# Weight sums of the gates' seven-product units: by adding DMAs for the first two units only, on DVE for the later four

## The chip, the cores and the metric

One core of one Trainium2 chip runs the whole kernel. The metric is the device time of one execution in microseconds (us). The engines are TensorE (PE, with its weight loads PEld), VectorE (DVE), ScalarE (ACT), GpSimd (POOL, which here issues adding DMAs) and SyncE (SP, which issues the other DMAs).

## What is computed

One block of a network on 512 tokens with 1024 channels, in fp32. The change touches only how the two gates are projected, the last two cuts of `proj`:

```
h = rms_norm(x, norm1_g[l])
proj = h @ w_in[l]
u_x, u_g, q, k, v, g_r, g_a = jnp.split(proj, cuts, axis=-1)
...
merged = (jax.nn.sigmoid(g_r) * (y_rnn @ w_br_rnn[l])
          + jax.nn.sigmoid(g_a) * (y_attn @ w_br_attn[l]))
x = x + merged @ w_out[l]
h2 = rms_norm(x, norm2_g[l])
x = x + jnp.square(jax.nn.relu(h2 @ w_mlp1[l])) @ w_mlp2[l]
```

Every product is held transposed (channels on the 128 partitions, 512 tokens along the row). To keep fp32 precision each operand is split in a high and a low part, and a product is three matmuls (high by high, high by low, low by high).

## The kernel before

**Units.** After attention and the recurrent branch the work is a list of units (`units()`). A unit is a pair of output chunks of 128 channels, with 1 MB of weights that SP loads as `raw`, four blocks of 128x512. The list around the change is: gr 0 and gr 2 (plain), four rnn units, then ga 0, gr 4, att 0, ga 2, gr 6, att 2, ga 4, att 4, ga 6, att 6, and then the output projection and the MLP ("one" and "two"). ga and gr are the two gates, att and rnn their branches.

**Seven products.** A plain unit splits its four blocks and uses them as four pieces. The units ga 0, gr 4, ga 2, gr 6, ga 4 and ga 6, and 14 units of the MLP, work as a 2x2 block product with seven multiplications in place of eight (`seven_products`). They use seven pieces: four blocks and three sums of blocks. The sums start from two: s1 = block 2 + block 3, and block 2 = block 2 + block 0. Later DVE makes block 0 + s1 (L220) and block 1 + block 0 (L222).

**Who makes the first two sums.** In the MLP DVE does (L217, L218), as the first piece of the unit is made. For the six gate units `load_unit` (L186 to L200) lets transfers do it: SP copies block 2 into s1 (L198), POOL issues one adding DMA of block 3 into s1 (L199) and one of block 0 into block 2 of `raw` (L200):

```
s1 = self.sums[u] = self.side[:, :T]
self.nc.sync.dma_start(s1, src[:, 2 * T:3 * T])
self.nc.gpsimd.dma_start(s1, src[:, 3 * T:], accum_op=ALU.add)
self.nc.gpsimd.dma_start(raw[:, 2], src[:, :T], accum_op=ALU.add)
```

All six share one tile, `side` (its name in the trace is pT): 512 columns for s1 and 256 for `uu`, the running difference of the products.

**Order.** `make_piece` asks for the loads of its unit and of the next one; `raw` has two buffers. Pieces are made eight ahead of their use on PE, in a ring of eight: ACT writes the high part (`whi`, L203), DVE the low part (`wlo`, L204). Since the next unit's load is asked for when a unit's first piece is made, and `side` is one tile, the copy and the add for gr 6 stand ahead of ga 2's first read of s1 in the program. So L220 of ga 2 waits for both units' transfers, and reads what gr 6's left there; gr 4 follows ga 0 in the same way. In the PE order a unit's first products are mixed with its neighbours' matmuls. The engines' orders are set by a scheduler.

**Products and their readers.** `seven_products` puts its products into four PSUM banks, in two tiles. ACT copies the first into `uu` (L266). DVE then reads the others: L268 (`uu`), L270, L272, L276 and L278 (into the unit's result `z`, S in the trace). PE's fourth product waits for L270, the sixth for L272 and the seventh for L276, since they write the tile that these read. The fifth needs no DVE reader.

Of the kernel before, what the change touches and what calls it, by code (L numbers as in the profile page):

```python
# [14 lines left out]
P = 128  # L15
T = 512
# [76 lines left out]
class Build:  # L93
# [93 lines left out]
    def load_unit(self, u):  # L187
        if u < len(self.units) and u not in self.raw_u:
            raw = self.t("raw", (P, 4, T), bufs=2)
            src = self.a["wts"][P1_END // 2 + u]  # L190
            self.nc.sync.dma_start(raw.rearrange("p c f -> p (c f)"), src)
            self.raw_u[u] = raw
            if self.units[u][0] in ("gr", "ga") and self.units[u][3]:

                if self.side is None:
                    self.side = self.t("pT", (P, T + H2))
# [4 lines that stand above are left out]
# [5 lines left out]
    def make_piece(self):  # L206
        V, n = self.nc.vector, self.made
        u, j = self.pieces[n]
        self.load_unit(u)
        self.load_unit(u + 1)  # L210
        raw = self.raw_u[u]
        blk = [raw[:, i] for i in range(4)]
        if self.units[u][3]:

            if j == 0 and u not in self.sums:
                s1 = self.sums[u] = self.t("pT", (P, T))
                V.tensor_tensor(s1, blk[2], blk[3], op=ALU.add)  # L217
                V.tensor_tensor(blk[2], blk[2], blk[0], op=ALU.add)  # L218
            elif j == 1:
                V.tensor_tensor(blk[0], blk[0], self.sums[u], op=ALU.add)  # L220
            elif j == 6:
                V.tensor_tensor(blk[1], blk[1], blk[0], op=ALU.add)  # L222
            src = (blk[0], blk[0], blk[2], self.sums[u], blk[1], blk[3], blk[1])[j]
        else:
            src = blk[j]
        s, e = n // 2 % (self.RING // 2), n % 2
        if n < self.RING and e == 0:
            self.ring_h.append(self.t("whi", (P, 2, T), FR, bufs=4))
            self.ring_l.append(self.t("wlo", (P, 2, T), FR, bufs=4))
        hi, lo = self.ring_h[s][:, e], self.ring_l[s][:, e]  # L230
        self.split_to(src, hi, lo)
        self.piece[n] = [x.rearrange("p (k m) -> p k m", m=P) for x in (hi, lo)]
        self.made += 1
# [804 lines left out]
```

## Time and profile before

| | |
|---|---|
| median of 3 runs | 891.11 us (890.53 to 893.37) |
| the profiled execution | 890.41 us, of which the span is 888.6 us |
| PE busy | 869.9 us, 98% of the span |
| DVE busy | 617.8 us, 70%, 1063 instructions |
| ACT busy | 494.4 us, 56% |
| POOL busy | 17.9 us, 2%, 25 instructions |
| chain that ended last | PE 91%, DVE 3%, ACT 2%, DMA 2% |

The span is the time from the first to the last instruction that the profile shows; the execution has 1.8 us around it. PE is the bound nearly everywhere, so what counts is where PE stands still, and at which clock it runs. TensorE's clock has two levels here, 2.4 GHz (1.00 in the PEclk column) and 1.2 GHz (0.50).

### The profile page before, as it was taken

Reading aid. Unit: us, or ns where it says so; the run is one execution under the profiler, and the core shown is the slowest. Engines: PE = TensorE matmul, PEld = TensorE weight load, DVE = VectorE, ACT = ScalarE, POOL = GpSimd, SP = SyncE. Lnnn points to the kernel's source line nnn. Section 1 sums busy time; section 2 is a strip of 40 time slices with the busy share of each in tenths; the row PEclk is TensorE's granted clock in tenths of the full one; section 3 lists DMA queues with packets and bytes.
Section 4 is the critical chain, followed back from the end, with each engine's and each line's share of the span. In section 5 each row is a group of like instructions: output and inputs, shape, how many; then the busy total and the mean of one; then the engine's idle time right before and its main releaser. Section 6 shows DMA issues by size and latency. Waiting matters only on the chain.

```text
span 888.6 us, 13051 instructions
## 1 busy us (share of the span) xinstructions
PE 869.9 (98%) x5033; PEld 744.0 (84%) x5033; DVE 617.8 (70%) x1063; ACT 494.4 (56%) x925; POOL 17.9 (2%) x25
## 2 busy tenths in 40 slices
PE   9999999999999999979999999999999999999996
PEld 7887788788787788968888889888888888888996
DVE  7777787795986866646765897776666666666533
ACT  7544856957868964524444546654444444444532
POOL 0000000000000012010000000000000000000000
PEclk9999999999999999989999999999999999999998
DMA  8443233134231357253436221222222222322211
GB/s 285 149 143 115 66 90 122 56 104 128 72 119 60 107 143 201 77 137 120 131 107 237 95 95 49 95 96 95 95 95 96 98 104 108 108 104 96 96 49 47
DMA packets 25645, 97.54 MB, mean 110 GB/s; under 512 B 3568, under 2 KB 6896, under 8 KB 16624
## 3 DMA queue, kind: packets, MB, share of 16 engines
q1 hardware_dynamic: 22704, 91.48, 29.8%
q0 software_dynamic: 2880, 5.24, 3.5%
q8 instruction: 39, 0.64, 0.3%
q14 instruction: 22, 0.18, 0.1%
HBM read 86.23 MB, written 2.10 MB: 99 GB/s over the span
## 4 chain that ended last, share of the span: by engine, by line
PE 91%; DVE 3%; ACT 2%; DMA 2%; issue 1%; SPq 0%; POOL 0%; DVEq 0%; ACTq 0%
PE pmm L248 38%; PE psc L248 22%; PE pmm L166 7%; PE pmm L167 7%; PE pmm L168 6%; PE psc L453 2%; PE pmm L453 2%; PE pmm L597 2%; PE psc L543 2%; DMA pT<-wts 1%; DMA S<-X 1%; PE ptr L581 1%; ACT L345 1%; ACT L L345 1%; DMA L<-xT 1%
## 5 line engine op out<-in xcount | busy, mean ns | idle before, releaser
L203 ACT CAST whi<-raw 128x512 fp32r<-128x512 f32 (+1 forms) x236 | 144.4, 626 | 212.5 <-PE pmm L248 101.0
L204 DVE TENSOR_TENSOR wlo<-raw,whi 128x512 fp32r<-128x512 f32 (+1 forms) x236 | 162.4, 697 | 55.6 <-ACT whi L203 52.7
L248 PE MATMUL psc<-X,whi 128*128 128x256 f32 x592 | 113.4, 289 | 6.4 <-DVE S L276 5.9
L248 PEld LDWEIGHTS psc<-X,whi 128*128 128x128 f32 x592 | 92.6, 190 | 14.1 <-DVE S L276 7.1
L248 PE MATMUL pmm<-E,whi 128*128 128x512 f32 x256 | 82.1, 396 | 0.3 <-ACT rot L345 0.3
L248 PE MATMUL psc<-X,wlo 128*128 128x256 f32 x296 | 81.5, 282 | 0.0
L166 PE MATMUL pmm<-X,whi 128*128 128x512 f32 x200 | 80.9, 405 | 0.0
L248 PE MATMUL pmm<-L,whi 128*128 128x512 f32 x256 | 80.5, 396 | 0.0
L167 PE MATMUL pmm<-X,whi 128*128 128x512 f32 x200 | 79.2, 396 | 0.0
L168 PE MATMUL pmm<-X,wlo 128*128 128x512 f32 x200 | 79.2, 396 | 0.0
L248 PE MATMUL psc<-Q,whi 128*128 128x256 f32 x320 | 70.1, 286 | 0.8 <-DVE tmp L268 0.8
L248 PEld LDWEIGHTS psc<-Q,whi 128*128 128x128 f32 x320 | 52.3, 188 | 6.4 <-DVE tmp L268 3.2
L248 PEld LDWEIGHTS pmm<-L,whi 128*128 128x128 f32 x256 | 48.0, 188 | 11.4
L248 PE MATMUL pmm<-B,whi 128*128 128x512 f32 (+1 forms) x224 | 57.5, 345 | 0.0
L248 PEld LDWEIGHTS pmm<-E,whi 128*128 128x128 f32 x256 | 47.6, 188 | 9.8 <-ACT rot L345 0.5
L248 PEld LDWEIGHTS psc<-X,wlo 128*128 128x128 f32 x296 | 55.5, 190 | 0.0
L248 PE MATMUL pmm<-V,whi 128*128 128x512 f32 (+1 forms) x192 | 54.6, 363 | 0.0
L248 PE MATMUL pmm<-L,wlo 128*128 128x512 f32 x128 | 50.8, 397 | 0.0
L248 PE MATMUL pmm<-E,wlo 128*128 128x512 f32 x128 | 50.7, 396 | 0.0
L136 ACT CAST whi<-raw 128x1024 fp32r<-128x1024 f32 (+1 forms) x36 | 34.3, 955 | 28.3 <-PE pmm L167 22.0
L166 PEld LDWEIGHTS pmm<-X,whi 128*128 128x128 f32 x200 | 37.7, 188 | 10.4 <-issue 1.5
L137 DVE TENSOR_TENSOR wlo<-raw,whi 128x1024 fp32r<-128x1024 f32 (+1 forms) x36 | 39.2, 1099 | 9.2 <-ACT whi L136 9.1
(312 smaller groups left out, 1876.3 us busy)
## 6 DMA issues: line engine op xcount, KB each, us to landing
raw<-wts SPq DMA_DIRECT2D x70, 1024.0 KB, 4.8
rot<-B SPq DMA_DIRECT2D x64, 64.0 KB, 2.0
L<-xT SPq DMA_DIRECT2D x8, 256.0 KB, 5.3
raw<-wts SPq DMA_DIRECT2D x8, 256.0 KB, 5.3
S<-X SPq DMA_DIRECT2D x8, 256.0 KB, 2.8
S<-X POOLq DMA_DIRECT2D x8, 256.0 KB, 4.5
R<-xT SPq DMA_DIRECT2D x8, 256.0 KB, 4.6
pT<-wts SPq DMA_DIRECT2D x6, 256.0 KB, 2.6
```

What stands on the lines that cost most here:

```text
L136: nc.scalar.copy(hf[:, s], raw[:, s])
L137: nc.vector.tensor_tensor(lf[:, s], raw[:, s], hf[:, s].bitcast(F), op=ALU.subtract)
L166: nc.tensor.matmul(ps, hi[:, k], xh[k], start=(k == 0), stop=False)
L167: nc.tensor.matmul(ps, hi[:, k], xl[k], start=False, stop=False)
L168: nc.tensor.matmul(ps, lo[:, k], xh[k], start=False, stop=(k == KT - 1))
L203: self.nc.scalar.copy(hi, src)
L204: self.nc.vector.tensor_tensor(lo, src, hi.bitcast(F), op=ALU.subtract)
L248: nc.tensor.matmul(out, l[:, k], r, start=((first if clear is None else clear) and k == 0 and g == 0), stop=(last and k == 3 and g == 2), ...
L345: ins = A.activation(*args, **kw).ins
L453: TE.matmul(pvs[half][i], xs[q][:, i * P:(i + 1) * P], (hv, lv)[wi][:, q % 2], start=(q == 0 and n == 0), stop=(q == KT - 1 and n == 2))
L543: ins = TE.matmul(scs[i - i0][:, m, :n], l[rows, 0, i * P:n], r[rows, 1, :n], start=(g == 0), stop=(g == len(terms_) - 1))
L597: TE.matmul(po[:, i], pdT[:, j], v[j][:, h * P:(h + 1) * P], start=(j == 0), stop=(j == i))
```

## The change

`load_unit` issues the three summing transfers only for ga 0 and gr 4. For ga 2, gr 6, ga 4 and ga 6 `make_piece` forms s1 and block 2 + block 0 on DVE, with the first piece, as it does for the MLP. The sum goes to the same columns of `side` as before.

```
-            if self.units[u][0] in ("gr", "ga") and self.units[u][3]:
+            if self.units[u][:2] in (("ga", 0), ("gr", 4)):
+
 
                 if self.side is None:
                     self.side = self.t("pT", (P, T + H2))
...
             if j == 0 and u not in self.sums:
-                s1 = self.sums[u] = self.t("pT", (P, T))
+                s1 = self.sums[u] = self.t("pT", (P, T)) if self.units[u][0] == "one" else self.side[:, :T]
                 V.tensor_tensor(s1, blk[2], blk[3], op=ALU.add)
                 V.tensor_tensor(blk[2], blk[2], blk[0], op=ALU.add)
```

Lines from L194 on have a number higher by one in the changed kernel (L217 becomes L218, L268 becomes L269). SP has four transfers fewer and POOL eight; DVE has eight additions more. Three places show what moves.

On DVE, while gr 4's products run and the pieces of ga 2 begin. raw_3316 holds att 0's weights, raw_3428 ga 2's; S_616 is gr 4's result. Before:

```order
L204 TENSOR_TENSOR wlo_2391<-raw_3316,whi_2390 128x512 x2
L272 TENSOR_TENSOR S_616_3427<-S_616_3427,psc_3314 128x256
L204 TENSOR_TENSOR wlo_2487<-raw_3428,whi_2486 128x512
L220 TENSOR_TENSOR raw_3428<-raw_3428,pT_3040 128x512
L276 TENSOR_TENSOR S_616_3427<-psc_3314,pT_3040 128x256
```

Now:

```order
L205 TENSOR_TENSOR wlo_2391<-raw_3316,whi_2390 128x512 x2
L218 TENSOR_TENSOR pT_3040<-raw_3428 128x512
L273 TENSOR_TENSOR S_616_3427<-S_616_3427,psc_3314 128x256
L219 TENSOR_TENSOR raw_3428<-raw_3428 128x512
L205 TENSOR_TENSOR wlo_2487<-raw_3428,whi_2486 128x512
L221 TENSOR_TENSOR raw_3428<-raw_3428,pT_3040 128x512
L277 TENSOR_TENSOR S_616_3427<-psc_3314,pT_3040 128x256
```

The two additions stand on either side of L273, and L221 now reads an s1 that DVE itself wrote. For gr 6 the same pair stands further down, behind L787 and between two wlo rows of ga 2.

On DVE, while ga 4's products run and the pieces of ga 6 begin. raw_3795 (now raw_3790) is att 4's weights, raw_3914 ga 6's; S_632 is ga 4's result. Before:

```order
L204 TENSOR_TENSOR wlo_2547<-raw_3795,whi_2546 128x512
L397 TENSOR_TENSOR E_631_3913<-S_623_3617,E_631_3913 128x512
L268 TENSOR_TENSOR pT_3040<-psc_3313,pT_3040 128x256
L270 TENSOR_TENSOR S_632_3916<-psc_3314,pT_3040 128x256
L204 TENSOR_TENSOR wlo_2547<-raw_3795,whi_2546 128x512
L204 TENSOR_TENSOR wlo_2621<-raw_3795,whi_2620 128x512
L272 TENSOR_TENSOR S_632_3916<-S_632_3916,psc_3314 128x256
```

Now:

```order
L205 TENSOR_TENSOR wlo_2547<-raw_3790,whi_2546 128x512
L398 TENSOR_TENSOR E_631_3910<-S_623_3613,E_631_3910 128x512
L218 TENSOR_TENSOR pT_3040<-raw_3914 128x512
L269 TENSOR_TENSOR pT_3040<-psc_3313,pT_3040 128x256
L205 TENSOR_TENSOR wlo_2547<-raw_3790,whi_2546 128x512
L271 TENSOR_TENSOR S_632_3913<-psc_3314,pT_3040 128x256
L205 TENSOR_TENSOR wlo_2621<-raw_3790,whi_2620 128x512
L219 TENSOR_TENSOR raw_3914<-raw_3914 128x512
L273 TENSOR_TENSOR S_632_3913<-S_632_3913,psc_3314 128x256
```

The addition into s1, which needs the whole load of ga 6, now stands ahead of L269 and L271, and a wlo row stands between these two.

On PE at the same place, from the end of ga 4's third product to its fourth (the R and Q rows behind the X rows). V is att 2's operand. Before:

```order
L248 MATMUL psc_3314<-R_609_3305,wlo_2621 128x256
L248 MATMUL pmm_4032<-V_567_2968,whi_2486 128x512
L248 MATMUL psc_3313<-X_83_468,whi_2390 128x256 x2
L248 MATMUL psc_3313<-X_83_468,wlo_2391 128x256
L248 MATMUL psc_3313<-X_84_469,whi_2390 128x256
L248 MATMUL psc_3314<-R_572_3015,whi_2620 128x256
```

Now:

```order
L249 MATMUL psc_3314<-R_609_3305,wlo_2621 128x256
L249 MATMUL pmm_4028<-V_567_2968,whi_2486 128x512 x2
L249 MATMUL psc_3313<-X_83_468,whi_2390 128x256 x2
L249 MATMUL psc_3313<-X_83_468,wlo_2391 128x256
L249 MATMUL psc_3313<-X_84_469,whi_2390 128x256 x2
L249 MATMUL psc_3313<-X_84_469,wlo_2391 128x256
L249 MATMUL psc_3313<-X_85_470,whi_2390 128x256
L249 MATMUL psc_3314<-R_572_3015,whi_2620 128x256
```

One V matmul and three X matmuls have moved ahead of the fourth product; they are missing behind it, and PE's work is the same in all.

## Rows read from the trace of the kernel before

**Rows 1.** The page's slices: TensorE's granted clock in 40 slices of 22.2 us.

```profile
PEclk9999999999999999989999999999999999999998
```

**Rows 2.** PE's waits over the whole span: total us, times, longest.

```profile
PE psc L248 <- DVE S L276: 5.9, 1, 5.9
PE ptr L320 <- DVE ebias L339: 1.5, 1, 1.5
```

**Rows 3.** The chain that ended last, 360 to 480 us: start us, us, what.

```profile
382.75 7.62 DMA pT<-wts
...
391.55 2.93 PE psc L248 x12
394.47 11.62 PE pmm L248 x44
...
448.44 1.53 PE psc L248 x12
449.97 10.25 PE pmm L248 x44
```

**Rows 4.** Stretches: length, busy time (x) of PE, PEld, DVE, ACT, POOL; PEclk, DMA share, GB/s.

```profile
390.00:390.50 0.50, 0.00 (x0) 0.00 (x0) 0.04 (x1) 0.00 (x0) 0.00 (x0) 1.00 0.98 160
...
391.55:397.26 5.71, 5.71 (x20) 5.03 (x20) 3.46 (x6) 1.88 (x4) 0.00 (x0) 0.50 0.00 0
520.00:830.00 310.00, 308.67 (x1981) 274.16 (x1980) 216.55 (x360) 158.36 (x287) 0.00 (x0) 1.00 0.28 100
```

**Rows 5.** DVE in order of time around the pause: start us, us, idle before it, releaser.

```profile
380.86 1.28 DVE L204 TENSOR_TENSOR wlo<-raw,whi 128x512 fp32r<-128x512 f32 x2
382.67 0.42 DVE L272 TENSOR_TENSOR S<-S,psc 128x256 f32<-128x256 f32 x1 [0.52 <-PE psc L248]
...
390.46 0.69 DVE L220 TENSOR_TENSOR raw<-raw,pT 128x512 f32<-128x512 f32 x1 [6.52 <-DMA pT<-wts]
...
398.20 0.69 DVE L204 TENSOR_TENSOR wlo<-raw,whi 128x512 fp32r<-128x512 f32 x1 [1.92 <-ACT whi L203]
```

**Rows 6.** SP's issues in order of time: ga 2's load, gr 6's, ga 4's and ga 6's come first.

```profile
375.74 0.33 SPq L191 DMA_DIRECT2D raw<-wts  x1
...
382.17 22.71 SPq L191 DMA_DIRECT2D raw<-wts  x2
...
416.80 7.10 SPq L191 DMA_DIRECT2D raw<-wts  x2
...
438.98 27.73 SPq L191 DMA_DIRECT2D raw<-wts  x4
```

**Rows 7.** Loads of 1 MB, us to landing, issued at 362.50, 375.74, 416.80 and 438.98.

```profile
raw<-wts SPq DMA_DIRECT2D x1, 1024.0 KB, 4.7
...
raw<-wts SPq DMA_DIRECT2D x1, 1024.0 KB, 5.8
...
raw<-wts SPq DMA_DIRECT2D x1, 1024.0 KB, 5.9
...
raw<-wts SPq DMA_DIRECT2D x1, 1024.0 KB, 5.1
```

**Rows 8.** L217, the MLP's addition into s1 on DVE: ns min/median/max; what its idle time awaited.

```profile
L217 DVE TENSOR_TENSOR pT<-raw x14: 684/692/694, 524.7 to 792.1; 128x512 f32<-128x512 f32 x14
...
  DMA raw<-wts: 4.8, 10
```

**Rows 9.** DVE and PE in order of time where ga 4's products meet ga 6's load.

```profile
422.26 1.28 DVE L204 TENSOR_TENSOR wlo<-raw,whi 128x512 fp32r<-128x512 f32 x2
...
441.49 0.69 DVE L397 TENSOR_TENSOR E<-S,E 128x512 fp32r<-128x512 f32 x1
442.70 0.43 DVE L268 TENSOR_TENSOR pT<-psc,pT 128x256 f32<-128x256 f32 x1 [0.52 <-PE psc L248]
443.24 0.42 DVE L270 TENSOR_TENSOR S<-psc,pT 128x256 f32<-128x256 f32 x1
...
443.77 0.33 PE L248 MATMUL psc<-R,whi 128*128 128x256 f32 x1
```

More of the change, by code (lines that the diff above doesn't have):

```diff
@@ L192, in load_unit @@
             self.raw_u[u] = raw
-            if self.units[u][0] in ("gr", "ga") and self.units[u][3]:
+            if self.units[u][:2] in (("ga", 0), ("gr", 4)):
                 if self.side is None:
@@ L215, in make_piece @@
             if j == 0 and u not in self.sums:
-                s1 = self.sums[u] = self.t("pT", (P, T))
+                s1 = self.sums[u] = self.t("pT", (P, T)) if self.units[u][0] == "one" else self.side[:, :T]
                 V.tensor_tensor(s1, blk[2], blk[3], op=ALU.add)
```

## The prediction, made before the changed kernel had run

> **What bounds the kernel now.** The page gives PE 98% of the span, so I looked for where PE stands still or runs slowly. The slices of the granted clock show full speed everywhere but in the slice that starts at 400 us and in the last one, where PE ends [rows 1]. The view of PE's waits has one wait of 5.9 us, on DVE's L276 [rows 2]; the next longest, 1.5 us, is at the kernel's start. So one place is special, and the chain of waits tells its cause [rows 3]: POOL's adding DMA into pT, issued at 382.75, takes 7.62 us, and only then do L220, L276 and PE go on, PE at 391.55. The wait of 5.87 us began at 385.68. DVE shows the same from its side: L220 of ga 2 sat 6.52 us for that DMA [rows 5]. By the program it is the sum for gr 6, the unit behind, since both use one tile.
>
> The clock comes second. It was still full in the 390.00 to 390.50 stretch, after PE had stood for 4.3 us, and then 0.50, 1.2 GHz, for the 5.71 us in which PE worked again [rows 4]. The other units of this phase show nothing of the kind.
>
> **What the change removes.** For ga 2 and gr 6 both transfers that L220 waited for are gone, so the wait goes: 5.87 us. With no pause the clock has no reason to fall. I take this from work that occurs twice: the 12 seventh-product matmuls and 44 plain ones behind the pause took 2.93 + 11.62 us, the same numbers of them at full clock 1.53 + 10.25 us [rows 3]. The difference is 2.77 us. (Half of the 5.71 us at half clock is 2.86, which agrees.) Together **8.6 us**. For ga 4 and ga 6 the transfers were hidden; there the change removes nothing that PE waited for. SP's four issues and POOL's eight lay beside other work; nothing is queued behind them that PE is waiting for.
>
> **What it adds.** Eight additions on DVE. The MLP has the same instruction: 692 ns by the median of 14 [rows 8], about 0.60 us of the engine's time when others follow at once, since a pair takes 1.28 [rows 5]. That is 4.8 to 5.5 us of DVE in a phase where it has gaps. What matters is what stands behind each pair, and whether the addition finds its load: it needs the whole 1 MB, where the transfers needed only their own 256 KB. I go by unit.
>
> ga 2: DVE is done with the two wlo rows at 382.06 (380.86 + 2 x 0.60). The load was issued at 375.74 [rows 6] and took 5.8 us [rows 7], so it is there by 381.54. s1 fits in ahead of L273, which in the trace starts at 382.67 because PE is not done sooner [rows 5]. Behind it come 0.34 for L273 and three rows of 0.60, so L277 starts near 385.0 and ends at 385.4, while PE came to it at 385.68. Cost 0; its cover is the 6.52 us that DVE idled, of which it needs about two.
>
> gr 6: its pair stands where DVE idled 1.92 us for ACT, from 396.28 to 398.20 [rows 5], in the new time 8.6 us earlier, from 387.7. The load, issued at 382.17 [rows 6], lands between 386.9 and 388.1 by the quickest and the slowest landing [rows 7]. A wait of 0.4 us and 1.2 us of work fit in the 1.92. PE then has the plain matmuls of att 0 to do, 10.25 us. Cost 0.
>
> ga 4: DVE comes to s1 at 423.46 [rows 9]; the load was issued at 416.80 [rows 6] and took 5.9 us [rows 7], there by 422.7. Cost 0, with 0.8 us to spare.
>
> ga 6: here it doesn't fit. s1 now stands ahead of L269 and L271, and PE's fourth product waits for L271. The load can't be issued sooner: its buffer comes free with ga 4's last piece, at 438.98 [rows 6]. Landing took 5.1 us there and 4.7 at the quickest [rows 7], so it is at 443.7 to 444.1. DVE is ready at 442.2 (441.49 + 0.69), stands, and so holds back L269, which started at 442.70, and L271, which ended at 443.66 [rows 9]. From the landing on come s1, L269, one wlo row and L271: at least 0.60 + 0.34 + 0.60 + 0.42 = 1.96 us, at most 0.69 + 0.43 + 0.69 + 0.42 = 2.23. So L271 ends between 445.6 and 446.3. PE reached this point at 443.77 [rows 9] and reaches it later now, since one V matmul (0.23 us, 10.25 over 44) and three X matmuls (0.12 each, [rows 3]) have moved ahead: 443.77 + 0.59 = 444.36. PE waits 1.3 to 2.0 us; I take **1.5**, nearer the lower end, since the POOL transfer that ran beside this load has gone. With a landing of 5.9 us it would be 2.8; if PE finds other cover, 0. The moved matmuls are missing further on, ahead of the sixth product: 0.1 us there.
>
> **The sum.** 890.41 - 8.6 + 1.5 + 0.1 = 883.4 us for an execution like the profiled one (span 881.6 and the 1.8 around it). The median of the runs was 0.7 above the profiled execution, so I predict **884.1 us**, a gain of 7.0 us or 0.8%.
>
> **A rule to weigh.** The clock stayed at 1.00 over 310 us of the MLP, in which DVE waited for a load ahead of s1 ten times for 4.8 us in all, and PE stood 1.3 us in all in many short waits [rows 4, 8]. The Trainium skill, "TensorE: Matmul & The Clock Gate", in the section on a second HAM failure mode, says that PE which idles briefly and often between groups of matmuls can swing between the two clock levels. The trace does not agree for such short waits, and has none of 1.5 us in such a phase. By that rule the new wait would cost the clock too, which is the third rival.
>
> **The rivals.** First: no new wait. If ga 6's load lands sooner or the scheduler's V and X matmuls cover it, all of the 8.6 remain: 882.5 us. For it speaks that the MLP has the same head-of-line addition with little harm [rows 8]; against, that the issue at 438.98 is tied to ga 4's last piece and DVE would be early by 1.5 us. Chance 0.15.
>
> Second: the pause only gets a new cause. DVE in order could stop for gr 6's load, with ga 2's pieces behind it; that landing is near 388, and if PE had nothing to do before, it would stand from 386 to 389 and lose half its clock again: about 3 + 2.8 us back, 1.5 at ga 6, so 889.9. Against it: att 0's four pieces are already in the ring when gr 6's turn comes, and they hold 10.25 us of matmuls. Chance 0.07, no measurable difference.
>
> Third: the new wait at ga 6 brings the low clock. Behind it PE has more than 10 us of matmuls, so it would lose another 2.8 us, as at the pause now: 886.9. Against it: the clock had still been full after 4.3 us of standing [rows 4]. Chance 0.12.
>
> Fourth, and slower: the additions wait for their load in each of the four units. s1 stands in front of L269 or L273 in three of them, and DVE is in order; if every load landed late enough for PE to stand 1.5 us and to fall to 1.2 GHz each time, that is 4 x (1.5 + 2.8) = 17.2 against 8.6: 899.7 us. It decides where the average loss per unit passes 2.2 us. For it: the spare time is only 0.5 us at ga 2 and 0.8 at ga 4. Against it: no landing of a 1 MB load in this phase took over 5.9 us, and the change takes away the transfers that competed with them. Chance 0.04.
>
> A case in which the change does nothing of what it says is excluded by the order: the twelve transfers are gone and the eight additions are there.
>
> **How the numbers follow.** The forecast, a gain of 5.8 to 7.5 us with the wait at ga 6, gets 0.62; with the rivals' 0.15, 0.07, 0.12 and 0.04 that is 1. About 0.3%, 2.7 us, is what a measurement of this kernel can tell from no change, so below 888.4 is faster: 0.62 + 0.15 + 0.12 = 0.89; within it 0.07; slower 0.04. The range must leave out no more than 0.2: it takes in the first rival, down to 881.6 (882.5 less 0.9, if the new runs lie nearer the profiled one), and the third with a late landing, up to 887.6 (886.9 and 0.7). Outside are the second and fourth.
>
> **What would show it.** Right: the wait of 5.9 us on L276 is gone from PE's waits, the clock is 1.00 at 385 to 398 us, and a new wait of 1 to 2 us on L271 stands near 436, with DVE idle before an L218 on the load of ga 6. A first step wrong: PE still stands near 386, with a raw load as the releaser. A second wrong: no wait on L271, or one followed by a stretch at 0.50. The forecast falls if the gain comes without the clock, or if waits on L273 show up at ga 2 or ga 4.

## The result, and the profile after

The changed kernel took 881.87 us by the median (881.26 to 882.91) against 891.1 us (890.53 to 893.37): a ratio of 0.9893, 95% interval 0.9872 to 0.9914, a gain of 9.2 us where 7.0 were forecast. Beside the experiments it ran twice more, on other chips: 883.23 us, ratio 0.9913 (0.9899 to 0.9928), and 882.32 us, ratio 0.9898 (0.9885 to 0.9912). It is faster by about 1%, 7.7 to 9.5 us by these ratios. The first measurement lies at the lower edge of my range, 881.6 us: a little inside by its median, a hair outside by its ratio (0.9893 of 891.11 is 881.57). What I missed is that the wait of 1.5 us which I had added at ga 6 never came.

The slices of the granted clock and PE's waits, which answer to [rows 1, 2]:

```profile
PEclk9999999999999999999999999999999999999998
```

```profile
PE ptr L321 <- DVE ebias L340: 1.5, 1, 1.5
PE ptr L378 <- ACT tmp L950: 0.8, 1, 0.8
...
PE psc L249 <- DVE S L273: 0.2, 1, 0.2
```

The 5.9 us are gone, nothing has come in their place, and only the last slice is below 9 now. The slice that was at 8 before is the one from 377.7 to 399.9 us (the 18th of 22.2 us each); the prediction has it start at 400 us, which is where it ends. The chain from 360 to 480 us, the place of [rows 3]:

```profile
379.93 4.46 PE psc L249 x36
384.39 0.70 PE pmm L249 x3
385.09 1.53 PE psc L249 x12
386.62 10.25 PE pmm L249 x44
...
433.88 0.47 PE pmm L249 x2
434.35 4.67 PE psc L249 x36
```

The 12 and 44 matmuls behind the former pause take 1.53 + 10.25 us, exactly what their twins took at full clock before [rows 3]. The chain no longer holds a DMA there. DVE in order of time at ga 2 (to [rows 5]):

```profile
380.82 0.69 DVE L205 TENSOR_TENSOR wlo<-raw,whi 128x512 fp32r<-128x512 f32 x1
381.42 0.69 DVE L218 TENSOR_TENSOR pT<-raw 128x512 f32<-128x512 f32 x1
382.08 0.42 DVE L273 TENSOR_TENSOR S<-S,psc 128x256 f32<-128x256 f32 x1
382.42 0.68 DVE L219 TENSOR_TENSOR raw<-raw 128x512 f32<-128x512 f32 x1
383.02 0.69 DVE L205 TENSOR_TENSOR wlo<-raw,whi 128x512 fp32r<-128x512 f32 x1
383.74 0.69 DVE L221 TENSOR_TENSOR raw<-raw,pT 128x512 f32<-128x512 f32 x1
384.43 0.42 DVE L277 TENSOR_TENSOR S<-psc,pT 128x256 f32<-128x256 f32 x1
```

Seven rows without idle time, and L277 ends at 384.85, before PE comes to the seventh product at 385.09. This is the step at ga 2 as it was worked out, 0.6 us earlier because this execution came to the units 0.6 us earlier.

The start is worth a caution. All kernels here have the same code up to rnn 6, yet PE reaches the last transposes ahead of ga 0 at 363.3 to 365.2 us, even for the same kernel (363.31, 365.06 and 363.74 in three executions of the change). So differences of about 1 us between single executions say nothing, and I compare the gates' stage by itself: from these transposes (L626, L627 in the change) to the start of the last matmul of ga 6's products. For the kernel before and the first execution of the change these are the lines

```profile
363.91 0.60 PE L626 MATMUL ptr<-ident,Q 128*128 128x128 f32 x4
471.19 0.28 PE L248 MATMUL psc<-X,wlo 128*128 128x256 f32 x1
```

```profile
363.31 0.60 PE L627 MATMUL ptr<-ident,Q 128*128 128x128 f32 x4
462.20 0.28 PE L249 MATMUL psc<-X,wlo 128*128 128x256 f32 x1
```

so 107.28 and 98.89 us. A table from the traces (two or three numbers in a row are runs of the same kernel):

| kernel | stage, us | median, us | ratio to before |
|---|---|---|---|
| before | 107.28 | 891.1 | |
| the change, three executions | 98.89, 99.06, 98.81 | 881.87, 883.23, 882.32 | 0.9893, 0.9913, 0.9898 |
| ga 2 and gr 6 on DVE | 98.59, 98.49 | 882.56, 882.1 | 0.9914, 0.9898 |
| ga 4 and ga 6 on DVE | 107.53 | 890.85 | 1.0004 |
| ga 4 alone by DMA | 100.35, 100.67 | 882.55, 883.46 | 0.9913, 0.9918 |
| all six on DVE | 98.79 | 882.85 | 0.9916 |
| s1 by DMA, block 2 on DVE | 104.20 | 888.85 | 0.9976 |
| s1 on DVE, block 2 by DMA | 100.60 | 883.78 | 0.9921 |
| gr 6 alone on DVE | 99.32 | 883.09 | 0.9913 |

The change shortens the stage by 8.2 to 8.5 us.

### The profile page after: what moved, and what is told of

It is laid out like the page before. It is cut to its first block, busy times and chain, and to the rows that moved or that the text cites. A ratio compares the mean times of both kernels' runs of the same rounds, so it can differ in the third digit from the quotient of the medians.

```text
span 879.5 us, 13019 instructions
## 1 busy us (share of the span) xinstructions
PE 867.0 (99%) x5033; PEld 742.4 (84%) x5033; DVE 623.1 (71%) x1071; ACT 495.0 (56%) x925; POOL 11.0 (1%) x17
## 4 chain that ended last, share of the span: by engine, by line
PE 92%; ACT 3%; DVE 3%; DMA 1%; issue 1%; SPq 0%; POOL 0%; DVEq 0%; ACTq 0%
PE pmm L249 38%; PE psc L249 22%; PE pmm L166 7%; PE pmm L167 7%; PE pmm L168 7%; PE pmm L454 3%; PE psc L454 3%; PE pmm L598 2%; PE psc L544 2%; DMA S<-X 1%; PE ptr L582 1%; ACT L346 1%; ACT L L346 1%; PE psc L659 0%; PE ptr L385 0%
```

## The experiments

**Where the gain is: ga 2 and gr 6, or ga 4 and ga 6.** The list of units that keep adding DMAs, against the change:

```
-            if self.units[u][:2] in (("ga", 0), ("gr", 4)):
+            if self.units[u][:2] in (("ga", 0), ("gr", 4), ("ga", 4), ("ga", 6)):
```

> Only ga 2 and gr 6 form their sums on DVE; ga 4 and ga 6 keep their adding DMAs, as do ga 0 and gr 4. Theory: the whole gain is the pause at ga 2 (5.9 us of standing and 2.8 us of half clock), so this run is at 881.5 to 883, like the change. Rival: a part of the gain comes from ga 4 and ga 6, whose transfers held ACT and DVE for 3.4 us each: then 884 to 888.

Measured: 882.56 us, ratio 0.9914 (0.9899 to 0.9929), no wait of PE over 0.2 us in the stage. The other half, with `("ga", 2), ("gr", 6)` in the list in place of `("ga", 4), ("ga", 6)`:

> Only ga 4 and ga 6 form their sums on DVE; ga 0, gr 4, ga 2 and gr 6 keep the adding DMAs. Theory: nothing gained, 890 to 892, with PE's wait of 5.9 us on the reader in front of the seventh product still there and the clock at half behind it. Rival: 885 to 889.

Measured: 890.85 us, ratio 1.0004 (0.9995 to 1.0013), and the old pause with its clock:

```profile
PE psc L249 <- DVE S L277: 5.9, 1, 5.9
```

```profile
385.40:391.20 5.80, 0.01 (x1) 0.00 (x0) 0.99 (x3) 0.83 (x2) 0.86 (x1) 0.92 0.98 203
391.25:396.96 5.71, 5.67 (x19) 5.04 (x20) 3.51 (x6) 1.93 (x4) 0.00 (x0) 0.50 0.00 0
```

All of the gain is at ga 2 and gr 6. Moving ga 4 and ga 6 too brings nothing, and the stage is 0.2 to 0.6 us longer with it. The kernel with only ga 2 and gr 6 on DVE, once more beside the change:

> Again the kernel with only ga 2 and gr 6 on DVE. Theory: ga 4 and ga 6 on DVE bring nothing, so the median is within 0.6 us of the change's in this call, on either side. Rival: more than 0.8 us slower than the change, a gain at ga 4 and ga 6.

> The change on a third chip, in five rounds, as the measure for the two runs beside it: 882 to 883.3, no wait of PE over 0.2 us between 330 and 480 us.

Measured: 882.1 us for ga 2 and gr 6 alone and 882.32 us for the whole change, with the same ratio, 0.9898 (0.9885 to 0.9912).

**What the pause hung on: the shared tile, POOL's queue, or the slowness of an adding DMA.** First gr 6 alone on DVE, with `("ga", 2), ("ga", 4), ("ga", 6)` added to the list:

> Only gr 6 forms its sums on DVE; ga 2 keeps its adding DMAs, so the tile holds ga 2's own sum when ga 2 reads it. Theory: the pause came from the neighbour's sum in the shared tile; ga 2's own sum had landed by 379.1 us, so the pause is gone: 881.5 to 884. Rival: an adding DMA is too slow for ga 2 whoever shares the tile; then PE still waits 3 us or more near 386 and the time is 887 to 891.

Measured: 883.09 us, ratio 0.9913 (0.9898 to 0.9928). Though ga 2's sums still come by adding DMAs, DVE's L221 no longer waits for one:

```profile
383.21 0.69 DVE L205 TENSOR_TENSOR wlo<-raw,whi 128x512 fp32r<-128x512 f32 x1 [0.16 <-ACT whi L204]
383.93 0.69 DVE L221 TENSOR_TENSOR raw<-raw,pT 128x512 f32<-128x512 f32 x1
384.99 0.42 DVE L277 TENSOR_TENSOR S<-psc,pT 128x256 f32<-128x256 f32 x1 [0.36 <-PE psc L249]
```

So the neighbour's sum in the shared tile was the cause, not the adding DMA as such: ACT still stood 3.21 us for ga 2's block 2 here, and PE did not stop there.

```profile
388.55 0.62 ACT L204 CAST whi<-raw 128x512 fp32r<-128x512 f32 x1 [3.21 <-DMA raw<-wts]
```

```profile
402.45 0.51 PE L249 MATMUL psc<-X,whi 128*128 128x256 f32 x2 [0.56 <-DVE pT L269]
```

PE waited 0.56 us at 402.45. That may be a late effect, since DVE stood 3.14 us behind that cast and had only 0.69 us of idle time from there to L269; no run tests it.

One thing besides the time: since ga 2 read gr 6's sum in the kernel before, the change also alters what ga 2's gate is computed from (its own sum now). ga 0 still reads gr 4's sum in the changed kernel; only the run with all six on DVE ends that too.

Then s1 by DMA for all six, with only the sum into block 2 moved to DVE (all six units stand in the list of the first line):

```
...
-                self.nc.gpsimd.dma_start(raw[:, 2], src[:, :T], accum_op=ALU.add)
+                if self.units[u][:2] in (("ga", 0), ("gr", 4)):
+                    self.nc.gpsimd.dma_start(raw[:, 2], src[:, :T], accum_op=ALU.add)
...
+            elif j == 0 and self.units[u][0] != "one" and self.units[u][:2] not in (("ga", 0), ("gr", 4)):
+                V.tensor_tensor(blk[2], blk[2], blk[0], op=ALU.add)
```

> For ga 2, gr 6, ga 4 and ga 6 only the sum into block 2 moves to DVE; s1 is still copied and added by DMA into the one tile. Theory: the pause hangs on s1 of gr 6 in the shared tile, so it stays: its adding DMA starts at most 0.5 us sooner and still runs beside the 1 MB load; PE waits 3.5 to 5.5 us and the time is 887 to 891. Rival: POOL's add into block 2, which stood ahead of it in POOL's queue, is what made it late: then 882 to 884.

Measured: 888.85 us, ratio 0.9976 (0.9966 to 0.9986); the pause stays, at 3.93 us, with the DMA into pT as DVE's releaser:

```profile
390.44 0.79 PE L252 MATMUL psc<-X,whi 128*128 128x256 f32 x2 [3.93 <-DVE S L280]
```

```profile
389.36 0.69 DVE L224 TENSOR_TENSOR raw<-raw,pT 128x512 f32<-128x512 f32 x1 [4.60 <-DMA pT<-wts]
```

The order of POOL's queue was not the cause of the pause: without the add into block 2 it is 1.9 us shorter (5.87 to 3.93), not gone. It is shorter because the transfer for gr 6 took 5.3 us to land here in place of 7.62 us [rows 3]; counted from the last transposes it was issued 0.4 us later, not earlier. Why it landed sooner is open. POOL's other add was gone, but the transfer was also issued 1.0 us behind the 1 MB load (383.95 and 382.94), where it had been 0.6 us before, and ga 4's add in the kernel before took 7.0 us with no other adding DMA beside it (shown further down).

Last the reverse, s1 on DVE and block 2 by an adding DMA that POOL issues behind s1:

```
...
-                V.tensor_tensor(blk[2], blk[2], blk[0], op=ALU.add)
+                if self.units[u][0] == "one":
+                    V.tensor_tensor(blk[2], blk[2], blk[0], op=ALU.add)
+                else:
+                    src = self.a["wts"][P1_END // 2 + u]
+                    self.nc.gpsimd.dma_start(raw[:, 2], src[:, :T], accum_op=ALU.add)
```

> For the same four units only s1 moves to DVE; the add of block 0 into block 2 stays an adding DMA, issued behind s1. Theory: no pause at ga 2, the clock stays full; ga 4's adding DMA still holds ACT, so the load of ga 6 is late and PE waits 0.8 to 2 us on the reader of its third product: 882.7 to 884.5. Rival: ACT, held by the late block 2 at ga 2, starves the ring and PE stands there: 885 to 890.

Measured: 883.78 us, ratio 0.9921 (0.9906 to 0.9936). No pause at ga 2, but the wait that I had predicted for the change, 1.36 us at ga 6:

```profile
436.70 0.51 PE L254 MATMUL psc<-X,whi 128*128 128x256 f32 x2 [1.36 <-DVE pT L274]
```

**Why the wait at ga 6 did not come.** This is the direct test: the change, but ga 4 keeps its DMAs (`("ga", 4)` added to the list).

> Like the change, but ga 4 keeps its adding DMAs (ga 2, gr 6 and ga 6 on DVE). Theory on the step that failed: ga 4's adding DMA into block 2 lands late, holds ACT and with it ga 4's last pieces, so the buffer of ga 6's load comes free about 1.9 us later, and the wait that the prediction saw appears: DVE idle 1 to 2.5 us ahead of the addition into s1 of ga 6, PE waiting 0.8 to 2 us on L271, 882.7 to 884. Rival: the load's issue does not hang on that DMA; then there is no such wait and the time is the change's, 881.3 to 882.5.

Measured: 882.55 us, ratio 0.9913 (0.9896 to 0.9929), a time that alone decides nothing: it is 0.15 us below what the theory gave, and three of the four executions lie at 882.48 to 882.59, like the kernel with only ga 2 and gr 6 on DVE beside them (882.56). The profiled one took 884.11 us, and its trace has the wait. DVE, PE, ACT and SP there:

```profile
433.76 0.70 DVE L398 TENSOR_TENSOR E<-S,E 128x512 fp32r<-128x512 f32 x1
436.23 0.69 DVE L218 TENSOR_TENSOR pT<-raw 128x512 f32<-128x512 f32 x1 [1.78 <-DMA raw<-wts]
436.84 0.42 DVE L269 TENSOR_TENSOR pT<-psc,pT 128x256 f32<-128x256 f32 x1
```

```profile
437.31 0.50 PE L249 MATMUL psc<-X,whi 128*128 128x256 f32 x2 [1.43 <-DVE pT L269]
```

```profile
422.57 0.62 ACT L204 CAST whi<-raw 128x512 fp32r<-128x512 f32 x1 [3.45 <-DMA raw<-wts]
```

```profile
431.25 0.33 SPq L191 DMA_DIRECT2D raw<-wts  x1
```

ACT stands 3.45 us for ga 4's block 2, its remaining pieces are late, and ga 6's load is issued at 431.25, 1.8 us later than in the change when both are counted from the last transposes; DVE then stands for it ahead of s1. The run before this one, which keeps only the add into block 2 as a DMA, has the same wait, so the add into block 2 is enough for it. Again beside the change:

> Again the kernel in which ga 4 alone of the four keeps its adding DMAs. Theory: the wait of about 1.4 us behind the late load of ga 6 is there in every execution and nothing later gives it back, so the median is 1.0 to 1.8 us above the change's in this call. Rival: it is made up elsewhere or there only in some executions: within 0.5 us of the change.

Measured: 883.46 us (883.25 to 884.85) against 882.32 us, 1.1 us more, and the wait again, 1.62 us:

```profile
436.34 0.51 PE L249 MATMUL psc<-X,whi 128*128 128x256 f32 x2 [1.62 <-DVE pT L269]
```

The slowest execution of the change here, 882.51 us, is below the quickest of these, 883.25, so the wait is paid at the end of the kernel too. Whether the three executions at 882.5 above had it is not known.

**All six on DVE.** The block of `load_unit` that issues the DMAs is taken out; `side` is still allocated there.

> All six gate units form their sums on DVE; no adding DMA for weights at all. Theory: ga 0's and gr 4's transfers are hidden behind the rnn units, so nothing changes by more than 0.5 us: 881.3 to 882.5. Rival: DVE, which is busier there with the splits and sums of the gates' input, makes PE wait: 883 to 886.

Measured: 882.85 us, ratio 0.9916 (0.9901 to 0.9931), no new wait of PE over 0.2 us near ga 0 and gr 4. The median is 0.35 us above what was expected and just below the rival's range, but the stage, 98.79 us, is as short as the change's. Their transfers were hidden, and the additions are hidden as well; it is no faster than the change.

**The change beside these.**

> The change itself once more, beside the runs of this call: 881.3 to 882.9, without a wait of PE over 0.2 us between 330 and 480 us.

Measured: 883.23 us, 0.3 us above the expected range and 1.4 us over its first run, though its stage is nearly as short (99.06 and 98.89 us); this execution came to the units at 365.06 us, 1.75 later than the first.

## Why the prediction was right in its cause and missed a term

**What bounds, and what goes: right.** The pause and its half clock were forecast at 5.87 + 2.77 = 8.6 us. With ga 2 and gr 6 alone on DVE the stage is 8.7 to 8.8 us shorter, and that is the whole gain. That the neighbour's sum in the shared tile was the cause is shown by the run with gr 6 alone.

**ga 2, gr 6, ga 4 at no cost: right.** None of their additions had idle time ahead for a load. What ga 4 and ga 6 cost besides is in the 0.2 to 0.6 us by which the change's stage exceeds that of ga 2 and gr 6 alone. PE stands still 0.31 to 0.33 us of the stage in all five traces, so the difference is in its busy time (98.49 to 98.75 us against 98.17 and 98.26); why, is open.

**ga 6: wrong.** The step that failed is "the load can't be issued sooner: its buffer comes free with ga 4's last piece, at 438.98". The buffer does come free with that piece, but the time of the piece was not PE's. In the kernel before, POOL's adding DMA into ga 4's block 2 was issued at 423.25 and took 7.0 us to land, and ACT's next cast started at 430.30:

```profile
423.25 0.86 POOL L200 DMA_DIRECT2D raw<-wts  x1 [7.60 <-DVE wlo L204]
...
430.30 0.62 ACT L203 CAST whi<-raw 128x512 fp32r<-128x512 f32 x1 [3.47 <-PE pmm L248]
```

```profile
raw<-wts POOLq DMA_DIRECT2D x1, 256.0 KB, 7.0
```

The view puts the 3.47 us down to PE, and I had passed over the row; 423.25 + 7.0 = 430.25 names the DMA. That delay ran on through ga 4's last pieces to the load of ga 6, and the change takes the DMA away. I had written of ga 4 and ga 6 that the change removes nothing that PE waited for, which is so, and had not asked what else waited for it. In the changed kernel SP, the load and DVE show:

```profile
427.91 0.33 SPq L191 DMA_DIRECT2D raw<-wts  x1
```

```profile
raw<-wts SPq DMA_DIRECT2D x1, 1024.0 KB, 4.6
```

```profile
432.29 0.69 DVE L398 TENSOR_TENSOR E<-S,E 128x512 fp32r<-128x512 f32 x1
432.90 0.69 DVE L218 TENSOR_TENSOR pT<-raw 128x512 f32<-128x512 f32 x1
```

DVE's row ahead of s1 moved by 9.2 us (441.49 [rows 9] to 432.29), the issue by 11.07 (438.98 [rows 6] to 427.91), so the load was issued 1.9 us sooner relative to DVE's work. It took 4.6 us to land, so it was there at 432.5, when DVE was still busy with L398 (until 432.9), and s1 started without a wait. What I had put at 1.5 us was 0, but its size was right for the case in which the DMA stays: 1.36, 1.43 and 1.62 us in the three traces that have it, against 1.3 to 2.0 worked out. It was the fifth product (the X rows) that waited, for L269, not the fourth for L271: the X matmuls that the scheduler had moved forward, and that I counted as cover, stand behind the same DVE row. I had described the fifth as needing no DVE reader; it writes the tile that L269 reads.

**The rivals.** The first, no new wait, is what happened; I gave it 0.15, because I took the issue time as fixed. The third is settled by the run with ga 4 by DMA: the clock stayed at 1.00 in the 7.70 us behind its wait of 1.43 us, and for 7.7 and 7.6 us behind the waits of 1.36 and 1.62 us in the other two traces.

```profile
437.30:445.00 7.70, 7.68 (x55) 7.07 (x56) 6.19 (x12) 3.48 (x7) 0.00 (x0) 1.00 0.39 136
```

What the Trainium skill ("TensorE: Matmul & The Clock Gate", in the section on a second HAM failure mode) says is about PE idling briefly and often. A single wait does not test that; the nearest that a trace here has are the many short waits of the MLP in the kernel before, with the clock at 1.00 [rows 4]. The second and the fourth rival fell: s1 found its load in all four units.

**The range.** Its lower end, 881.6, was the first rival less 0.9 us for the scatter of executions. The first measurement lies at that edge, a hair outside by its ratio and inside by its median; the two later ones lie inside it. That it went so low is in part luck: its 9.2 us are more than the 8.2 to 8.5 us that the stage gained, and the profiled execution reached the units 0.6 us sooner than the one before, ahead of anything that the change touches. Without the false term I would have said 882.5.

## What to carry to other kernels

A time that is read from a trace and kept as fixed ("the buffer comes free at ...") must itself be followed back to what set it, through the engines that are not the bound: here two steps back it was one of the very transfers that the change removes. Where a wait's releaser in the view had long been busy with other things, compare the end of the idle time with the landings of DMAs. And a tile that two neighbouring units share makes the first wait for the second's transfers as soon as those are asked for ahead of its reads; moving only the second unit's sum off the transfers was enough to end the pause.

## What was not expected of the hardware

TensorE's clock fell earlier in one run than in another. In the kernel before it was still 1.00 when PE had stood for 4.3 us [rows 4]. In the run with s1 by DMA PE stopped at 386.51, the clock was full up to 389.50 and half from 390.00 on:

```profile
386.50:389.50 3.00, 0.01 (x1) 0.00 (x0) 0.14 (x1) 0.00 (x0) 0.00 (x0) 1.00 0.69 156
389.50:390.00 0.50, 0.00 (x0) 0.00 (x0) 0.50 (x2) 0.00 (x0) 0.00 (x0) 0.94 0.00 0
390.00:390.40 0.40, 0.00 (x0) 0.00 (x0) 0.40 (x3) 0.26 (x1) 0.00 (x0) 0.50 0.00 0
390.44:393.20 2.76, 2.76 (x13) 2.76 (x14) 1.75 (x3) 0.85 (x2) 0.00 (x0) 0.50 0.00 0
```

So the 4.3 us of the one trace, which I used against the third rival, were no bound. Its length differed too: the clock was back at 393.4 us in this run, and the 12 and 44 matmuls behind the pause lost 1.4 us (2.93 + 10.29 against 1.53 + 10.25) where they had lost 2.77.

How long an adding DMA of 256 KB took to land went with the 1 MB load beside it. In the kernel before it took 3.7 us with no such load on its way (issued at 322.12), and 7.0 us when a load followed 0.3 us later (423.25 and 423.57), with no second adding DMA near. With a load and a second adding DMA beside it, it took 7.0 and 7.6 us (382.15 and 382.75). In the run with s1 by DMA, issued 1.0 us behind a load and without a second one, it took 5.3 us. So a second adding DMA is not needed for a landing of 7 us; what else sets it, no run here separates.
